# Reordering the state-space and the recurrent layer of a four-layer float32 program, and holding each layer's first weight splits behind the second token tile's copy

## The chip, the core and the metric

The program runs on one core of a Trainium2 chip. TensorE (PE) multiplies, with its weight loads on a row of their own (PEld); VectorE (DVE), ScalarE (ACT) and GpSimd (POOL) do the elementwise work, and SyncE (SP) issues the transfers from HBM. The metric is the device time of one execution, in microseconds.

## What is computed

256 tokens of width 1024 go through a first block (attention and a mixture of 16 experts) and a second block of four layers. Only the second block is touched: a state-space layer (SSD), a convolutional feed-forward layer (FFN 0), a gated linear recurrence (LRU) and FFN 1. All of it is float32. Cut to what matters:

```python
# SSD, 4 groups of 8 heads, 2 chunks of 128 tokens
cs = cumsum(dt * a); decay_in = exp(cs[l] - cs[s]) below the diagonal
y  = (C B^T * decay_in) @ (x*dt) + (C @ state) * exp(cs) + d_skip * x
g  = y * silu(z); g *= rsqrt(mean(g*g, over the 512 columns of a group)) * w
out = g @ w_out
# LRU, 10 blocks of 128 columns
x = dwconv(proj_x); gx, ga = sigmoid(blockwise x @ w_gx + b), sigmoid(x @ w_ga + b)
log_a = 8 * ga * log_sigmoid(lam); a = exp(log_a); m = sqrt(-expm1(2*log_a))
h_t = a_t * h_(t-1) + m_t * gx_t * x_t; out = (h * gelu(proj_y)) @ w_out + b_out
```

## The kernel before

Weights come in pages of 1 MB (128x2048 float32) into five slots, by SP, in the order in which the program asks for them. A matrix product takes both factors apart into two float32r tiles, a high and a low part, and adds three products (`three`, L234 to L236). `split` does this for a page: ACT copies the high part (`wh`, L222), DVE subtracts (`wl`, L223); three slots hold split pages. `c_proj` multiplies one page of 256 columns (48 PE products of 256 columns), `down` one page of an output projection (24 products of 512 columns into four accumulators `ca`). Two PSUM tags `cm` and `cs` with two buffers each take all else.

Between layers, `next_layer` (L1192) normalizes each of two token tiles of 128 tokens: sums of squares on ACT, scaling, and then `turned` (L1136): eight PE transposes, a copy of one half on ACT and of the other on DVE (`hf`, L1143), the products of the next layer's first two pages directly in float32 (`lead`, L1149), and the high parts on ACT (L1152) and low parts on POOL (L1153) of the activations.

In `ssd` (L1332) the step sizes go through `softplus` (L1272, a POOL chain of some 20 small instructions); four pages give B and C, two pages per group give x (`x_group`) and two z (`z_group`). `scan(g)` (L1416) builds decays for four heads at a time: `csb` (L1442) spreads a cumulative sum over partitions by float32 products with a triangle of ones, one for each head; DVE or ACT subtract, ACT takes the exponential, DVE multiplies, PE forms `y`. `scan_end(g)` multiplies by silu(z) on POOL (L1483), squares on ACT (L1484), sums by PE (`ssq`, L1488), takes the root in 13 small DVE steps, spreads it by PE (`rb`) and splits the result (`ys`), its low part on POOL. `out_group(g)` is the output projection. The order of the text is: for each g, scan(g), x_group(g+1), z_group(g), scan_end(g), out_group(g-1).

In `lru` (L1517) four small products put the output bias into the accumulators (L1531), `softplus` runs over `lambda`; five pages give x, each followed by its convolution and by `gates` of the page before (L1544: two PE products on each of two gates, tanh and sigmoid on ACT, DVE); five pages give y. Then, in five pieces, exp and tanh on ACT, a square on POOL (L1593), one root for all (L1595), and for each piece a product, two scans (L1600), gelu (L1601) and a product on DVE; the split has its low part on POOL. Five `down` pages follow, the last three in one call.

The queue of an engine is not the text's order: the framework plans, by its own estimates of durations, which instruction of an engine comes next, with earlier text first among those that it takes to be ready. Each engine then runs its queue strictly in order. `tc.issue_after(i)` makes the planner put an instruction behind `i` in the queue of the same engine. The weight pages of later text can so be split ahead.

Of the kernel before, what the change touches and what calls it, by code (L numbers as in the profile page):

```python
# [9 lines left out]
F32 = mybir.dt.float32  # L10
# [25 lines left out]
for _n, _k in COLS:  # L36
# [8 lines left out]
    ("ident", 128), ("one", 1), ("iota", 256), ("tok", 2), ("tri", 128), ("eye16", 16),  # L45
]
# [14 lines left out]
def constants():  # L61
# [24 lines left out]
    put("eye16", (p == np.arange(16)[None]).astype(np.float32))  # L86
    put("one", np.ones((128, 1), np.float32))
# [77 lines left out]
def tile_model(ctx, tc, A, out):  # L165
# [970 lines left out]
    def turned(t, xg, hf, hi, lo, lead):  # L1136

        os_ = [(slice(None), slice(4 * b, 4 * b + 4), nat(t)) for b in range(2)]
        for b in range(2):
# [3 lines left out]
            (act.copy, dve.tensor_copy)[b](hf[os_[b]], ps.rearrange("p (k n) -> p k n", k=4))  # L1143
# [150 lines left out]

    lru_lead = [lambda j=j: wpage(A["lru_w_in_2"][0], 1280 + 256 * j, 256) for j in range(2)]
# [36 lines left out]
    def ssd(hx, acc_, led):  # L1332
        with ExitStack() as es:
# [6 lines left out]
            da = sp2.tile([128, 2, 32], F32, name="da")  # L1340
# [13 lines left out]
            u = sp2.tile([128, 64], F32, name="dtu")  # L1354
            dve.tensor_copy(u, ps[:, :64])
            r = softplus(sp2, u, [128, 64], "sp")
            pool.tensor_copy(dt, r.rearrange("p (t h) -> p t h", t=2))
            pool.tensor_tensor(da, dt, na[:, None, :].to_broadcast([128, 2, 32]), ALU.mult)
# [35 lines left out]
            for t in range(2):  # L1394
                with tc.issue_after(last_mm[0].ins):
                    pe.matmul(ps[:, 32 * t:32 * t + 32], lhsT=K("tri"), rhs=da[:, t], start=True, stop=True)
            pe.matmul(ps[:, 64:96], lhsT=K("one").to_broadcast([128, 128]), rhs=da[:, 0], start=True, stop=True)
            dve.tensor_copy(csn, ps[:, :64].rearrange("p (t h) -> p t h", t=2))
            dec = sp2.tile([128, 32], F32, name="dec")
# [16 lines left out]
            def scan(g):  # L1416
# [18 lines left out]
                for q in range(2):  # L1435
# [43 lines left out]
            def scan_end(g):  # L1479
                sq = xs[g]  # L1480
                for q in range(2):
                    qs = slice(2 * q, 2 * q + 2)
                    pool.tensor_tensor(zs[g][:, qs], zs[g][:, qs], xs[g][:, qs], ALU.mult)  # L1483
# [11 lines left out]
                for c in range(4):  # L1495
                    dve.scalar_tensor_tensor(zs[g][:, c], zs[g][:, c], C("ssd_norm_2", 4 * g + c), rb[:, :256],
                                             ALU.mult, ALU.mult)
                ys[g] = split(zs[g], sp3, "ys", 2, pool)
# [5 lines left out]

            for g in range(4):
# [11 lines left out]
    def lru(hx, led):  # L1517
        with ExitStack() as es:
# [8 lines left out]
            for n in range(2):  # L1527
                b_out = lp.tile([128, 2 * S], F32, name="b_out", tag="raw", bufs=2)[:1]
                sync.dma_start(out=b_out, in_=A["lru_b_out_2"][:, 512 * n:512 * n + 512])
# [7 lines left out]
            hb = lp.tile([128, 20], F32, name="hb")  # L1537
            dve.tensor_scalar(hb[:, :10], C("lru_b_gx_2", 0, 10), 0.5, None, ALU.mult)
            xb = lp.tile([128, 10, S], F32, name="xb")
            yb = ly.tile([128, 10, S], F32, name="yb")  # L1540
            gx = lp.tile([128, 10, S], F32, name="gx")
            la = lp.tile([128, 10, S], F32, name="la")

            def gates(i):  # L1544
                for j, g in enumerate((gx, la)):
                    ps = cs("lgate")
                    for c in range(2):
                        ch = 2 * i + c
                        pe.matmul(ps[:, 256 * c:256 * c + 256], lhsT=wg[j][:, ch], rhs=xb[:, ch], start=True, stop=True)  # L1549
                    for c in range(2):  # L1550
                        ch = 2 * i + c
                        p_ = ps[:, 256 * c:256 * c + 256]
                        if j == 0:

                            act.activation(out=gx[:, ch], in_=p_, func=AF.Tanh, scale=0.5, bias=hb[:, ch:ch + 1])
                            dve.scalar_tensor_tensor(gx[:, ch], gx[:, ch], 1.0, xb[:, ch], ALU.add, ALU.mult)
                        else:
                            act.activation(out=la[:, ch], in_=p_, func=AF.Sigmoid, bias=C("lru_b_ga_2", ch))
                            dve.tensor_scalar(la[:, ch], la[:, ch], ls[:, ch:ch + 1], None, ALU.mult)

            for i in range(5):
# [9 lines left out]
                conv2(xb[:, 2 * i:2 * i + 2], raw, lambda c, a: C("lru_conv_w_2", 10 * a + 2 * i + c),  # L1571
                      lambda c: C("lru_conv_b_2", 2 * i + c), 4)
                if i:
                    gates(i - 1)

            def y_page(i):
                ps = cm("ly")
                c_proj(wpage(w, 256 * i, 256), ps, hx)
                for c in range(2):
                    ch = 2 * i + c  # L1580
                    dve.tensor_scalar(yb[:, ch], ps[:, 256 * c:256 * c + 256], C("lru_b_in_2", ch), None, ALU.add)

            y_page(0)
# [11 lines left out]
            act.activation(out=la, in_=la, func=AF.Sqrt)  # L1595
            for o in range(0, 10, 2):
                os_ = slice(o, o + 2)
                dve.scalar_tensor_tensor(gx[:, os_], gx[:, os_], 0.5, la[:, os_], ALU.mult, ALU.mult)
                for ch in (o, o + 1):
                    dve.tensor_tensor_scan(la[:, ch], xb[:, ch], gx[:, ch], 0.0, ALU.mult, ALU.add)  # L1600
                act.activation(out=yb[:, os_], in_=yb[:, os_], func=AF.Gelu_apprx_tanh)  # L1601
                dve.tensor_tensor(yb[:, os_], yb[:, os_], la[:, os_], ALU.mult)
            items = []
            for b in range(5):
                pr_ = split(yb[:, 2 * b:2 * b + 2], ly, "ls", 3, pool)
                items.append((rpage(A["lru_w_out_2"][0], 256 * b), [sl(pr_, lambda u: u[:, a]) for a in range(2)]))
                if b < 2:
                    down(acc_, [items.pop()], False, False)
            es2.close()
            lp = es.enter_context(tc.tile_pool(name="lru_out", bufs=1, reuse_waits="tile"))  # L1610
            root_table(lp, pr_[0].bitcast(F32)[:, 0, 0:1])
            down(acc_, items, False, True, lp)
# [29 lines left out]
```

## Time and profile before

| | us |
|---|---|
| median of 3 runs (2313.93 to 2317.94) | 2314.22 |
| the profiled execution, its own time | 2311.94 |
| its span, first to last instruction | 2310.1 |
| first block (to the end of the experts) | 0 to 1386 |
| SSD, with the passage into it | 1386 to 1634 |
| passage and FFN 0 | 1634 to 1910 |
| passage into LRU, LRU | 1910 to 2028 |
| passage and FFN 1 | 2028 to 2310 |

The span is 1.84 us shorter than the profiled execution's time, and that execution is 2.28 us below the median. A window view gives the busy time of each engine in a stretch and, under PEclk, TensorE's granted clock as a share of 2.4 GHz (0.50 is 1.2 GHz). Records of PE overlap, since matmuls are pipelined; the pace of a stream is read from the distance of starts.

### The profile page before, as it was taken

What the parts mean: (1) busy time and instruction counts of PE and PEld (TensorE: products, weight loads), DVE (VectorE), ACT (ScalarE), POOL (GpSimd) and SP (SyncE); (2) the same over time, 40 slices, a digit from 0 to 9 for tenths busy, and PEclk for the clock granted to TensorE, in tenths of its full rate; (3) what the DMA queues carried; (4) which work ended last, traced back from release to release, by engine and by line L of the source; (5) the groups of instructions that cost most, each with busy time, mean ns of one, the idle gap of its engine ahead of it and who ended that gap; (6) DMA issues with size and microseconds to landing.
All of it is one profiled execution on the core that took longest, in us unless ns stands there. A gap on an engine that the chain in (4) does not pass through costs nothing. (4 is left out here: it accounts for less than half of the span.)

```text
span 2310.1 us, 30319 instructions
## 1 busy us (share of the span) xinstructions
PE 1921.2 (83%) x12819; PEld 1341.3 (58%) x12819; DVE 996.5 (43%) x1473; ACT 806.4 (35%) x1190; POOL 268.8 (12%) x209
## 2 busy tenths in 40 slices
PE   7999999988665656656565669999999999899998
PEld 5989999933111111111111118887888888788887
DVE  8866664331000000000000007765677766777775
ACT  3445454311000000000000006664666667666664
POOL 0100032100000000000000003112322222222221
PEclk9999999999878787877888789999999999999999
DMA  9357666699999999999999997333466546456562
GB/s 321 109 188 262 227 219 203 238 372 427 426 427 426 425 428 426 427 426 427 425 428 426 427 414 250 103 111 127 148 199 192 188 149 206 146 175 190 184 199 82
DMA packets 211167, 645.22 MB, mean 279 GB/s; under 512 B 8148, under 2 KB 162132, under 8 KB 178390
## 3 DMA queue, kind: packets, MB, share of 16 engines
q1 hardware_dynamic: 211032, 643.28, 73.5%
q8 instruction: 101, 1.65, 0.3%
q14 instruction: 34, 0.28, 0.0%
HBM read 641.94 MB, written 1.05 MB: 278 GB/s over the span
## 5 line engine op out<-in xcount | busy, mean ns | idle before, releaser
L223 DVE TENSOR_TENSOR wl<-page,wh 128x2048 fp32r<-128x2048 f32 (+2 forms) x191 | 436.3, 2286 | 207.1 <-ACT wh L222 206.9
L1084 PE MATMUL gu<-epage,xeT 128*32 128x512 f32 x2048 | 318.4, 739 | 198.0 <-DMA epage<-in_w_gu 198.0
L222 ACT CAST wh<-page 128x2048 fp32r<-128x2048 f32 (+2 forms) x191 | 356.9, 1873 | 174.9 <-issue 46.2
L1236 PE MATMUL up<-hb,wh 128*128 128x512 f32 x960 | 331.6, 396 | 0.0
L1084 PEld LDWEIGHTS gu<-epage,xeT 128*32 128x32 f32 x2048 | 60.9, 123 | 435.2 <-DMA epage<-in_w_gu 326.0
L1087 ACT ACTIVATE hid<-gu 128x512 f32<-128x512 f32 x16 | 9.6, 597 | 786.6 <-PE gu L1084 786.6
L1105 PE MATMUL dn<-epage,hidT 128*32 128x512 f32 x1024 | 168.7, 788 | 104.4 <-DMA epage<-in_w_dn 95.5
L1239 PE MATMUL up<-hb,wl 128*128 128x256 f32 x960 | 248.0, 279 | 0.0
L1088 DVE TENSOR_TENSOR hid<-hid,gu 128x512 f32<-128x512 f32 x16 | 11.0, 688 | 490.6 <-PE gu L1084 490.6
L1236 PEld LDWEIGHTS up<-hb,wh 128*128 128x128 f32 x960 | 173.3, 188 | 33.4
L1239 PEld LDWEIGHTS up<-hb,wl 128*128 128x128 f32 x960 | 180.9, 188 | 10.4
L1105 PEld LDWEIGHTS dn<-epage,hidT 128*32 128x32 f32 x1024 | 31.5, 129 | 226.0 <-DMA epage<-in_w_dn 155.5
L1108 DVE TENSOR_TENSOR ye<-dn,gt 128x512 f32<-128x512 f32 x16 | 11.1, 692 | 286.9 <-PE dn L1105 286.9
L1269 DVE SCALAR_TENSOR_TENSOR cv<-ups,cols,cv 128x255 f32<-128x255 f32 x240 | 118.1, 502 | 28.8 <-ACT cv L1264 26.0
L278 POOL TENSOR_SCALAR iq<-ssq 128x1 f32<-128x1 f32 x16 | 8.0, 500 | 1002.0 <-ACT x L267 958.1
L234 PE MATMUL qk<-hh,wh 128*128 128x256 f32 x384 | 109.9, 286 | 0.0
L235 PE MATMUL qk<-hl,wh 128*128 128x256 f32 x384 | 109.0, 284 | 0.0
L236 PE MATMUL qk<-hh,wl 128*128 128x256 f32 x384 | 108.7, 283 | 0.0
L234 PE MATMUL ca<-wh,hdh 128*128 128x512 f32 x256 | 99.9, 390 | 0.0
L236 PE MATMUL ca<-wh,hdl 128*128 128x512 f32 x256 | 99.7, 390 | 0.0
L235 PE MATMUL ca<-wl,hdh 128*128 128x512 f32 x256 | 99.6, 389 | 0.0
L1264 ACT ACTIVATE cv<-ups,cols 128x256 f32<-128x256 f32 x120 | 71.1, 599 | 80.1 <-DVE ups L1244 79.9
(508 smaller groups left out, 3742.4 us busy)
## 6 DMA issues: line engine op xcount, KB each, us to landing
epage<-in_w_gu SPq DMA_DIRECT2D x102, 2048.0 KB, 29.5
epage<-in_w_dn SPq DMA_DIRECT2D x51, 2048.0 KB, 29.5
page<-in_ffn_w_up SPq DMA_DIRECT2D x64, 1024.0 KB, 5.6
epage<-in_w_gu SPq DMA_DIRECT2D x52, 1024.0 KB, 34.3
page<-in_w_in SPq DMA_DIRECT2D x46, 1024.0 KB, 5.7
page<-in_ffn_w_down SPq DMA_DIRECT2D x32, 1024.0 KB, 4.8
epage<-in_w_dn SPq DMA_DIRECT2D x26, 1024.0 KB, 34.3
page<-in_w_ada SPq DMA_DIRECT2D x24, 1024.0 KB, 8.9
```

The source lines that it names most:

```text
L222: act.copy(hi[p_], v[p_])
L223: (lo or dve).tensor_tensor(lw[p_], v[p_], hi[p_], ALU.subtract)
L234: pe.matmul(ps, lhsT=ah, rhs=bh, start=first and k == 0, stop=False)
L235: pe.matmul(ps, lhsT=ah, rhs=bl, start=False, stop=False)
L236: last_mm[0] = pe.matmul(ps, lhsT=al, rhs=bh, start=False, stop=last and k == n - 1)
L1084: pe.matmul(gu[i][32 * j:32 * j + 32, :], lhsT=xeT[:, k, 32 * e:32 * e + 32], rhs=pg[i][:, 512 * j:512 * j + 512], start=(k == 0), stop=(k ...
L1105: pe.matmul(pd[32 * q:32 * q + 32, :], lhsT=hT[:, 2 * c2 + cp, j, :], rhs=pg[c2][:, o:o + 512], start=(j == 0 and c2 == 0), stop=(j == 3 a ...
L1108: dve.tensor_tensor(ye, pd, gt2, ALU.mult)
L1236: wide = lambda: pe.matmul(ps, lhsT=wh[:, k, cc], rhs=hx[k][2], start=(k == 0), stop=(k == 7))
L1239: last_mm[0] = pe.matmul(ps[:, :256], lhsT=wl[:, k, cc], rhs=hx[k][0], start=False, stop=False)
L1264: act.activation(out=y[:, c], in_=ps[:, 256 * c:256 * c + 256], func=AF.Identity, scale=wcol(c, taps - 1), bias=bcol(c))
L1269: dve.scalar_tensor_tensor(y[:, c, o:], ps[:, 256 * c:256 * c + S - o], wcol(c, j), y[:, c, o:], ALU.mult, ALU.add)
```

## The change

- `split` issues the first three page splits after each passage behind ACT's `hf` copy of the second token tile.
- SSD: `z_group(0)` comes ahead of the first scan, and `z_group(g+1)` behind `scan_end(g)`; `out_group(0)` behind z_group(2), `out_group(1)` inside the last scan, `out_group(2)` behind the last scan_end. `csb` is one float32r product of 512 columns in place of four float32 ones; its right side is made once, ahead of the scans. The product with silu(z) goes from POOL to DVE, the normalized result has its own tile, and the last group's low part goes to DVE in two pieces.
- LRU: softplus of `lambda` is done in SSD's softplus, as ten more columns. The bias becomes four float32r products, behind the last gates. The gates come one projection later. The exponentials are queued behind the last sigmoid; the first three gelu pieces come at once behind the root, the last two y pages come behind it too, with gelu taken from PSUM. Square and low parts go from POOL to DVE.

```diff
+    behind_ = [None, 0]
     def split(v, pl=None, tag="w", bufs=None, lo=None, parts=1):
...
+        ahead = tag == "w" and behind_[1] > 0
+        behind_[1] -= ahead
         for i in range(parts):
-            act.copy(hi[p_], v[p_])
+            with tc.issue_after(behind_[0].ins) if ahead else ExitStack():
+                act.copy(hi[p_], v[p_])
             (lo or dve).tensor_tensor(lw[p_], v[p_], hi[p_], ALU.subtract)
@@ turned
-            (act.copy, dve.tensor_copy)[b](hf[os_[b]], ps.rearrange("p (k n) -> p k n", k=4))
+            c_ = (act.copy, dve.tensor_copy)[b](hf[os_[b]], ps.rearrange("p (k n) -> p k n", k=4))
+            if b == 0 and t == 1:
+                behind_[:] = [c_, 3]
@@ ssd
+            u = sp2.tile([128, 74], F32, name="dtu")
+            pool.tensor_scalar(u[:, 64:], C("lru_lambda_2", 0, 10), -1.0, None, ALU.mult)
...
+            r = softplus(sp2, u, [128, 74], "sp")
+            pool.tensor_scalar(lru_c[:, :10], r[:, 64:], -8.0, None, ALU.mult)
...
+            for t in range(2):
+                pr = cs("csr")[:, :128]
+                pe.matmul(pr, lhsT=da[:, t].rearrange("p a h -> p (a h)"), rhs=K("tri"), start=True, stop=True)
+                v_ = sp2.tile([128, 128], F32R, name="csv", tag="csv", bufs=2)
+                act.copy(v_, pr)
+                dve.tensor_tensor(v_[32:64], pr[32:64], v_[32:64], ALU.subtract)
+                bd = sp2.tile([128, 4, 128], F32R, name="csd", tag="csd", bufs=2)
+                dve.tensor_tensor(bd, v_[:, None, :].to_broadcast([128, 4, 128]),
+                                  K("mod4")[:, :, None].to_broadcast([128, 4, 128]), ALU.mult)
+                rows.append(bd.rearrange("p u l -> p (u l)"))
@@ scan
-                        for u_ in range(4):
-                            pe.matmul(ps[:, 128 * u_:128 * u_ + 128],
-                                      lhsT=da[:, t, hb + u_:hb + u_ + 1].to_broadcast([128, 128]), rhs=K("tri"),
-                                      start=True, stop=True)
+                        pe.matmul(ps, lhsT=of4[:, hb // 4:hb // 4 + 1].to_broadcast([128, 128]), rhs=rows[t],
+                                  start=True, stop=True)
@@ scan_end
-                    pool.tensor_tensor(zs[g][:, qs], zs[g][:, qs], xs[g][:, qs], ALU.mult)
+                    dve.tensor_tensor(zs[g][:, qs], zs[g][:, qs], xs[g][:, qs], ALU.mult)
...
-                ys[g] = split(zs[g], sp3, "ys", 2, pool)
+                ys[g] = split(sq, sp3, "ys", 2, dve if g == 3 else pool, parts=2 if g == 3 else 1)
@@ order of the groups
+            z_group(0)
             for g in range(4):
                 scan(g)
                 if g < 3:
                     x_group(g + 1)
-                z_group(g)
+                else:
+                    out_group(1)
                 scan_end(g)
-                if g:
-                    out_group(g - 1)
+                if g < 3:
+                    z_group(g + 1)
+                if g == 1:
+                    out_group(0)
+            out_group(2)
@@ lru
-                for t in range(2):
-                    pe.matmul(acc_[t][n], lhsT=K("one")[:1].to_broadcast([1, 128]), rhs=b_out, start=True, stop=False)
-            lam = lp.tile([128, 10], F32, name="lam")
-            dve.tensor_scalar(lam, C("lru_lambda_2", 0, 10), -1.0, None, ALU.mult)
-            ls = softplus(lp, lam, [128, 10], "lam")
-            dve.tensor_scalar(ls, ls, -8.0, None, ALU.mult)
+            def biases():
...
+                for n in range(2):
+                    for t in range(2):
+                        pe.matmul(acc_[t][n], lhsT=one_r, rhs=b_r[:, 512 * n:512 * n + 512], start=True, stop=False)
...
-                if i:
-                    gates(i - 1)
+                for j in {2: [0], 3: [1], 4: [2, 3]}.get(i, []):
+                    gates(j)
...
+            y_page(0, False)
             gates(4)
-            for i in range(1, 5):
-                y_page(i)
+            biases()
+            for i in range(1, 3):
+                y_page(i, False)
             for o in range(0, 10, 2):
                 os_ = slice(o, o + 2)
-                act.activation(out=xb[:, os_], in_=la[:, os_], func=AF.Exp)
+                with tc.issue_after(last_sig[0].ins):
+                    act.activation(out=xb[o // 2], in_=la[:, os_], func=AF.Exp)
...
-                pool.tensor_tensor(q, xb[:, os_], xb[:, os_], ALU.mult)
+                dve.tensor_tensor(q, xb[o // 2], xb[o // 2], ALU.mult)
...
+            root = act.activation(out=la, in_=la, func=AF.Sqrt)
+            with tc.issue_after(root.ins):
+                act.activation(out=yb[:, :6], in_=yb[:, :6], func=AF.Gelu_apprx_tanh)
...
+                if b > 2:
+                    y_page(b, True)
...
+                hi, lo = (lp.tile([128, 2, S], F32R, name="ls" + n, tag=n, bufs=5) for n in ("gx", "xb"))
+                act.copy(hi, yb[:, os_])
+                dve.tensor_tensor(lo, yb[:, os_], hi, ALU.subtract)
```

## Rows read from the trace of the kernel before

**Rows 1.** The page: each engine's busy time, share of the span, instructions

```profile
PE 1921.2 (83%) x12819; PEld 1341.3 (58%) x12819; DVE 996.5 (43%) x1473; ACT 806.4 (35%) x1190; POOL 268.8 (12%) x209
```

**Rows 2.** Windows by stage: stretch, its length, busy time by engine, PEclk, DMA share, GB/s

```profile
1386.00:1407.00 21.00, 17.23 (x120) 14.04 (x120) 15.35 (x19) 15.06 (x32) 9.37 (x12) 1.00 0.70 219
1442.00:1634.00 192.00, 181.03 (x1282) 159.19 (x1280) 118.62 (x218) 107.53 (x145) 31.49 (x14) 0.96 0.34 110
1910.00:1936.00 26.00, 22.55 (x156) 19.25 (x155) 13.84 (x19) 14.77 (x25) 10.78 (x24) 0.93 0.63 195
1936.00:1991.00 55.00, 54.90 (x425) 53.67 (x425) 47.34 (x77) 52.70 (x70) 8.17 (x6) 1.00 0.64 216
1991.00:2028.00 37.00, 30.07 (x120) 24.03 (x119) 25.76 (x28) 14.61 (x23) 7.36 (x8) 0.86 0.28 86
2028.00:2049.00 21.00, 18.45 (x147) 17.88 (x146) 13.80 (x13) 12.97 (x20) 7.28 (x5) 0.92 0.38 125
```

**Rows 3.** Waits of PE, 1442 to 1634: total us, times, longest

```profile
PE ssq L1488 <- ACT xs L1484: 6.9, 5, 2.0
```

**Rows 4.** Waits of PE, 1910 to 2049

```profile
PE ca L235 <- DVE wl L223: 6.9, 1, 6.9
PE lead L1149 <- DVE hf L1143: 3.1, 1, 3.1
PE lead L1149 <- ACT hf L1143: 2.9, 3, 2.2
```

**Rows 5.** Timeline of PE: start, us, instruction; the stream of csb, then one of 512 columns

```profile
1449.13 2.00 PE L1442 MATMUL csb<-kc,da 128*128 128x128 f32 x16
1450.89 0.36 PE L235 MATMUL xbc<-hb,wh 128*128 128x256 f32 x1
...
1888.47 0.39 PE L235 MATMUL ca<-wl,hdh 128*128 128x512 f32 x1
1888.70 0.39 PE L236 MATMUL ca<-wh,hdl 128*128 128x512 f32 x1
```

**Rows 6.** Groups by form, 1442 to 1634: busy us, mean ns, idle before, releasers

```profile
L223 DVE TENSOR_TENSOR wl<-page,wh 128x2048 fp32r<-128x2048 f32 x19 | 43.3, 2287 | 18.8 <-ACT wh L222 18.6
...
L1483 POOL TENSOR_TENSOR zs<-zs,xs 128x512 f32<-128x512 f32 x8 | 20.8, 2596 | 129.2 <-ACT zs L1384 106.6 <-ACT wh L222 13.1 <-DVE xs L1476 9.6
L1442 PE MATMUL csb<-kc,da 128*128 128x128 f32 x128 | 18.4, 282 | 0.0
...
L1454 DVE TENSOR_TENSOR scr<-scr,cb 128x512 f32<-128x512 f32 x16 | 11.0, 691 | 7.2 <-ACT scr L1453 7.0
L223 POOL TENSOR_TENSOR ysl<-zs,ysh 128x1024 fp32r<-128x1024 f32 x4 | 9.6, 2393 | 39.7 <-ACT ysh L222 20.0 <-issue 19.7
...
L1428 DVE TENSOR_TENSOR xd<-xdt,dec 128x512 f32<-128x512 f32 x4 | 4.7, 1169 | 0.0
```

**Rows 7.** Windows: the end of group 0, the clock in it, the scan of group 1

```profile
1467.00:1485.00 18.00, 16.04 (x121) 15.84 (x122) 7.72 (x17) 6.91 (x7) 4.16 (x2) 0.91 0.38 117
1481.00:1486.00 5.00, 5.00 (x32) 5.00 (x31) 2.57 (x13) 2.14 (x2) 0.00 (x0) 0.67 0.15 50
1485.00:1511.00 26.00, 24.39 (x208) 21.70 (x207) 21.57 (x38) 20.01 (x30) 3.65 (x2) 1.00 0.23 69
```

**Rows 8.** Timelines of ACT and DVE in three passages between layers

```profile
1400.83 0.58 ACT L1143 COPY hf<-tT 128x512 f32<-128x512 f32 x1 [2.56 <-PE tT L1142]
...
1923.26 1.21 DVE L1536 TENSOR_SCALAR r<-r 128x10 f32<-128x10 f32 x1 [5.04 <-POOL r L1289]
1924.39 0.68 DVE L1143 COPY hf<-tT 128x512 f32<-128x512 f32 x1
...
2035.80 3.68 ACT L222 CAST wh<-page 128x2048 fp32r<-128x2048 f32 x2
2039.39 0.57 ACT L1143 COPY hf<-tT 128x512 f32<-128x512 f32 x1
```

**Rows 9.** Group by form, 1910 to 2050: the bias products of LRU

```profile
L1531 PE MATMUL ca<-b_out,kc 1*128 1x512 f32 x8 | 4.0, 614 | 0.0
```

More of the change, by code (lines that the diff above doesn't have):

```diff
@@ L86, in constants @@
     put("eye16", (p == np.arange(16)[None]).astype(np.float32))
+    put("mod4", (p % 4 == np.arange(4)[None]).astype(np.float32))
+    put("of4", ((p < 64) & (p % 32 // 4 == np.arange(8)[None])).astype(np.float32))
     put("one", np.ones((128, 1), np.float32))
@@ L1293, in up_lead @@
         return [lambda j=j: wpage(A["ffn_w_up_2"][i], 4096 * j, 256) for j in range(2)]
+    lru_c = cp.tile([128, 20], F32, name="lru_c")
+    pool.tensor_scalar(lru_c[:, 10:], C("lru_b_gx_2", 0, 10), 0.5, None, ALU.mult)
     lru_lead = [lambda j=j: wpage(A["lru_w_in_2"][0], 1280 + 256 * j, 256) for j in range(2)]
@@ L1339, in ssd @@
             dt = sp2.tile([128, 2, 32], F32, name="dt")
-            da = sp2.tile([128, 2, 32], F32, name="da")
+            da = sp2.tile([128, 2, 4, 32], F32, name="da")
             ps = led[0]
@@ L1395, in ssd @@
                 with tc.issue_after(last_mm[0].ins):
-                    pe.matmul(ps[:, 32 * t:32 * t + 32], lhsT=K("tri"), rhs=da[:, t], start=True, stop=True)
-            pe.matmul(ps[:, 64:96], lhsT=K("one").to_broadcast([128, 128]), rhs=da[:, 0], start=True, stop=True)
+                    pe.matmul(ps[:, 32 * t:32 * t + 32], lhsT=K("tri"), rhs=da[:, t, 0], start=True, stop=True)
+            pe.matmul(ps[:, 64:96], lhsT=K("one").to_broadcast([128, 128]), rhs=da[:, 0, 0], start=True, stop=True)
             dve.tensor_copy(csn, ps[:, :64].rearrange("p (t h) -> p t h", t=2))
+            of4 = sp2.tile([128, 8], F32R, name="of4")
+            act.copy(of4, K("of4"))
+            rows = []
+            for t in range(2):
[8 more added lines that the diff above has]
+                rows.append(bd.rearrange("p u l -> p (u l)"))
             dec = sp2.tile([128, 32], F32, name="dec")
@@ L1526, in lru @@
             acc_ = accs()
[L1527 to L1539 removed]
+            ls, hb = lru_c[:, :10], lru_c[:, 10:]
+            def biases():
+                one_r = lp.tile([64, 128], F32R, name="one_r")
+                act.copy(one_r, K("one")[:64].to_broadcast([64, 128]))
+                b_out = lp.tile([64, D], F32, name="b_out")
+                pool.memset(b_out, 0.0)
+                for i in range(2):
+                    sync.dma_start(out=b_out[32 * i:32 * i + 1], in_=A["lru_b_out_2"])
+                b_r = lp.tile([64, D], F32R, name="b_r")
+                act.copy(b_r, b_out)
+                pool.tensor_tensor(b_r[32:64], b_out[32:64], b_r[32:64], ALU.subtract)
+                for n in range(2):
+                    for t in range(2):
+                        pe.matmul(acc_[t][n], lhsT=one_r, rhs=b_r[:, 512 * n:512 * n + 512], start=True, stop=False)
+            xb, gx = ([lp.tile([128, 2, S], F32, name=n, tag=n, bufs=5) for _ in range(5)] for n in ("xb", "gx"))
             yb = ly.tile([128, 10, S], F32, name="yb")
[L1541 removed]
             la = lp.tile([128, 10, S], F32, name="la")
+            last_sig = [None]
             def gates(i):
[L1545 removed]
+                for j in range(2):
                     ps = cs("lgate")
@@ L1548, in gates @@
                         ch = 2 * i + c
-                        pe.matmul(ps[:, 256 * c:256 * c + 256], lhsT=wg[j][:, ch], rhs=xb[:, ch], start=True, stop=True)
+                        with tc.issue_after(last_mm[0].ins):
+                            pe.matmul(ps[:, 256 * c:256 * c + 256], lhsT=wg[j][:, ch], rhs=xb[i][:, c], start=True, stop=True)
                     for c in range(2):
@@ L1580, in y_page @@
                     ch = 2 * i + c
-                    dve.tensor_scalar(yb[:, ch], ps[:, 256 * c:256 * c + 256], C("lru_b_in_2", ch), None, ALU.add)
-            y_page(0)
+                    p_, b_ = ps[:, 256 * c:256 * c + 256], C("lru_b_in_2", ch)
+                    if gelu:
+                        act.activation(out=yb[:, ch], in_=p_, func=AF.Gelu_apprx_tanh, bias=b_)
+                    else:
+                        dve.tensor_scalar(yb[:, ch], p_, b_, None, ALU.add)
+            y_page(0, False)
@@ L1609, in lru @@
+            item = lambda b: (rpage(A["lru_w_out_2"][0], 256 * b), [sl(pr_[b], lambda u: u[:, a]) for a in range(2)])
+            for b in range(2):
+                down(acc_, [item(b)], False, False)
+            root_table(cp, pr_[4][0].bitcast(F32)[:, 0, 0:1])
+            down(acc_, [item(b) for b in range(2, 5)], False, True)
             es2.close()
-            lp = es.enter_context(tc.tile_pool(name="lru_out", bufs=1, reuse_waits="tile"))
-            root_table(lp, pr_[0].bitcast(F32)[:, 0, 0:1])
```

42 lines of the change are left out of this document (18 added, 24 removed).

## The prediction

> **What bounds the kernel now.** The page comes first [rows 1]: PE is busy for 83% of the span, DVE 43%, ACT 35%, so it is PE's idle time and its slow stretches that can be won, and PE's own work. The windows by stage say where they lie [rows 2]. From 1936 to 1991, in the middle of LRU, PE is busy 54.90 of 55 us at full clock: nothing is to be had there but fewer products. SSD (192 us) has 11.0 us without PE, and a granted clock of 0.96. The end of LRU (37 us) has 6.9 us without PE at 0.86. The two passages around LRU have 3.5 and 2.6 us without PE at 0.93 and 0.92. The waits of PE name the causes: in SSD the squares of a group's end come late (6.9 us in five waits) [rows 3]; in LRU one wait of 6.9 us for the low part of a page, 3.1 us for DVE's copy in the passage into it, and 2.9 us for ACT's copies, of which 2.2 us at one go [rows 4]. A wait costs more than itself: after the idle time in group 0's end the clock falls to 0.67 for five microseconds [rows 7], which is 5 x 0.33 = 1.7 us more.
>
> A change of under 0.2% (4.6 us) can't be told from none here.
>
> **Part by part.**
>
> **csb.** Sixteen records start between 1449.13 and 1450.89, one each 0.11 us [rows 5]; 128 of them [rows 6] take 14.1 us of PE. Sixteen products of 512 columns, at 0.23 us between starts [rows 5], take 3.7. Making the right side adds four records of 128 columns: 0.4. Net 10.0. PE is busy 181 of 192 us there [rows 2], so I take 94% of it: **-9.4** (ends -5 and -10). The other new steps are three ACT copies and four DVE instructions, each bounded by 0.69 us, the DVE product of 512 elements [rows 6], 4.8 us in all. They lie between the last B/C page and the first csb, beside the products of z's first two pages (96 x 0.12 = 11.5 us, at half of the 0.23); without that cover they would cost their 4.8.
>
> **The end of a group.** POOL takes 2.60 us for half of the product with silu(z), DVE 0.69 for that shape [rows 6]. The last half is on the way to the squares, so 1.9 us go at each of four ends, about what each wait is long (2.0 at most) [rows 3]. With the wait goes the slow stretch: 6.9 us and four times 1.7 make 13.5. SSD's idle time and lost clock together are 11.0 + 192 x 0.04 = 18.7 [rows 2], so there is room for that. The next that can be late is the chain of roots behind the squares; it then has z_group(g+1) beside it (11.5 us of PE), and in the last group out_group(2) (48 x 0.23 = 11). I take **-12** (ends -4, where the next link waits, and -16).
>
> First the row: DVE's `xd`, a product of the 0.69 us kind, takes 1.17 us in the mean of four [rows 6], which are 1.9 us too many in all. The Trainium skill, in "SBUF — State Buffer", section "Who interferes with whom", says that a DVE instruction with two SBUF inputs waits for a whole GpSimd instruction that reads SBUF. By that rule a moved product that met one of the three low parts left on POOL (2.39 us each) would wait for it, at most 7.2 us together, and the sum below would be 24.7 in place of 31.9.
>
> **DVE's new load, and the scans' lost cover.** DVE gets eight products (5.5 us), the last group's low part (two of 0.69) and the 2.8 us of above: 9.7 us on top of 118.6 in 192. That is hidden on the whole, but not evenly. The scan of group 1 now takes 26 us, DVE 21.6 of them [rows 7], and PE had two x and two z pages beside it. After the change z stands behind scan_end: the scan has some 6 us of PE of its own (an estimate: the stretch's 24.4 less 0.9 a csb stream saved and four pages' products as far as they lie in it) and two x pages, 11.5, so 17.5 us against about 22 of DVE. Four scans lose 0 us if the planner pulls z's products ahead (two `cm` buffers and three split slots allow one group) and 4.5 each, 18, if it doesn't. In the trace a later page's product stands right behind the csb stream [rows 5], so I take a value nearer to nothing: **+5**.
>
> **Holding the splits.** Three ACT copies a passage are queued behind `hf`; behind them stand the tile's two casts, then the first product of the layer. In the passage into SSD: hf from 1400.83 for 0.58 [rows 8], two casts of as much, 1.84 for the copy (two in 3.68) [rows 8], 2.29 for the low part [rows 6]: 1406.7. PE is meanwhile on 48 float32 products of the lead pages ((120 - 8 - 16)/2 records [rows 2], 5.3 us at 0.11) until about 1407; in the other passages on 64, 7 us. So the hold costs 0 (end: 2 us each, where DVE or the `softplus` feed comes between). A page slot comes free up to 5 us later, so its transfer does too, but PE needs 5.8 us (48 x 0.12) for each held page, and the DMA share is 0.28 to 0.70 in these stretches [rows 2]: nothing.
>
> **Passage into LRU.** DVE's `hf` copy stands behind the last step of softplus, which waits 5.0 us for POOL's chain [rows 8]; softplus now runs in SSD, where its POOL chain only gets ten columns more and two small instructions. The 3.1 us wait goes, and with it the lost clock (26 x 0.07 = 1.8). Eight records of the bias take 4.0 us [rows 9]; four products of 512 columns take 0.9, later: 3.1. Together 8.0, I take **-7** (ends -5 and -8). Its transfers move behind y's first page on SP, two short rows; POOL clears and subtracts beside 24 us of PE.
>
> **LRU's middle.** Gates one projection later and fewer table loads on ACT (52.7 of 55 busy) win nothing while PE is full [rows 2]: **0**.
>
> **LRU's end.** 120 products at 0.23 are 27.6 of the 37 us: 9.4 us lost to the late page split and the half clock behind it. DVE was the one that came late. It loses the stretched products beside POOL and four of ten bias additions, and gets five squares and five low parts (10 x 0.69). ACT loads the gelu table once. But y's fourth and fifth page now stand behind the root. I take about half: **-5** (ends 0 and -9).
>
> **Passage into FFN 1.** Two page copies (3.68 us) stand ahead of `hf` [rows 8] and PE waits 2.2 us [rows 4]; with the clock (21 x 0.08 = 1.7) that is 3.9. Held, they are gone from there: **-3.5** (ends -2 and -4). Into FFN 0 ACT had idle time for them; 0.
>
> **Sum.** -9.4 - 12 + 5 + 0 - 7 + 0 - 5 - 3.5 = -31.9 us against the profiled execution, 2311.94: 2280.0. That execution lies 2.28 below the median, so 2282.
>
> **The rivals.**
>
> **The scans become DVE's.** The +5 is +18, and SSD wins 3.4 instead of 16.4: 2295. For it: DVE at 21.6 of 26 us with the same x pages [rows 7]. Against it: csb comes 0.6 us sooner four times a scan, and DVE is busy just 7.7 of 18 us in a group's end, so there is room to shift its work. The Trainium skill, in "Perfetto Trace Analysis", section "Optimizing Scalar/DVE Operations", speaks against the move too: where DVE is saturated, work should rather go to ScalarE or GpSimd, and between DVE and GpSimd moving may not help. The trace agrees for the scans and not for the ends. Chance 0.20.
>
> **The new order isn't what is queued.** The planner orders by its own estimates, so the moved groups may stand where they stood; only replaced instructions count: csb 9.4, the passage into LRU 7. 2298. Chance 0.08.
>
> **Slower: PE stands still in every scan.** If each scan, with x alone beside it, is stretched to the sum of its DVE work and ACT's links, some 30 us (22 + 8), SSD from 1442 to 1634 becomes: z 11.5, four scans 120, four ends 18 - 3.8 = 14.2 each, two output groups outside 22, eight slow restarts of 1.7: 224 against 192 plus the 6 ahead of it. That is +26, less 15.5 of LRU: +10.5, 2325 at the median. It decides from 27 us a scan on (with LRU's gain used up). For it: the queues are in order, so one late DVE result stops PE with pages ready behind it. Against it: 26 us now, with more DVE work inside [rows 7]. Chance 0.08.
>
> **How the numbers follow.** The forecast has 0.64: 2282, its own range 2267 (all good ends: 10 + 16 + 8 + 9 + 4 = 47) to 2292. To leave out no more than 2 in 10, the range goes up to the two rivals at 2295 and 2298 with a little of their bad ends: 2267 to 2301. Faster by over 0.2%: 0.64, 0.16 of the DVE rival and 0.07 of the order rival, 0.87. Within 0.2%: the bad ends of these two, 0.05. Slower: 0.08.
>
> **What would show it.** In the profile after: 16 csb records of 512 columns 0.23 apart; no wait of `ssq` for ACT, and SSD's clock at 0.98 or more; SSD's stretch shorter by 16 us; the passage into LRU near 18 us without the wait for `hf`; LRU's end at 32; no page copy ahead of `hf` in any passage. Wrong would be: waits of PE for `scr` or `xd` in the scans with DVE full (the first rival); first products of a layer waiting for `wl` (the hold costs); a new wait in LRU for the low part of y's fourth page.

## The result, and the profile after the change

The changed kernel takes 2276.41 us (median of four runs, 2275.1 to 2277.32) against 2315.3 for the kernel before beside it: a ratio of 0.9831, 95% interval 0.9819 to 0.9842, so it is faster by 38.9 us. The profiled executions, on which the sum was made, are 2311.94 and 2275.1: 36.8 us, where 31.9 were forecast.

The first 1393 us are the same code but for one POOL instruction of 0.3 us, so I cut the rest at PE's records, from the first record of one tile to the first of the next. Profiles of code that is alike in a stage agree on most middle and late stages within 0.2 us: FFN 0 takes 257.29 to 257.33 in ten of them, SSD's body 176.6 in the five that leave it alone and keep its clock. LRU's middle is looser (56.1 to 56.5, and 57.4 in run 3, which does not touch it), the start of the transposes into SSD lies anywhere from 1393.2 to 1398.6, and the passage into SSD takes 13.8 to 15.2. So the stages, not the totals, carry the readings below.

| stage (us) | before | after | difference | forecast |
|---|---|---|---|---|
| up to the transposes into SSD | 1393.2 | 1393.7 | +0.5 | 0 |
| passage into SSD | 13.8 | 13.8 | 0 | 0 |
| to the running sums (`csn`) | 29.1 | 29.5 | +0.4 | 0 |
| SSD's body, to the transposes into FFN 0 | 200.0 | 176.6 | -23.3 | -16.4 |
| passage into FFN 0, to `up` | 19.0 | 17.0 | -2.0 | 0 |
| FFN 0 | 255.1 | 257.3 | +2.2 | 0 |
| passage into LRU, to `lx` | 25.5 | 17.1 | -8.4 | -7 |
| LRU's middle, to the last product of y | 55.0 | 56.2 | +1.2 | 0 |
| LRU's end | 37.5 | 31.3 | -6.2 | -5 |
| passage into FFN 1 | 20.7 | 17.1 | -3.6 | -3.5 |
| FFN 1, to its last product | 254.9 | 257.1 | +2.2 | 0 |
| the rest | 6.4 | 6.5 | +0.2 | 0 |

The windows by stage of the changed kernel, as in [rows 2] (stretch, length, busy time of PE, PEld, DVE, ACT, POOL, PEclk, DMA share, GB/s):

```profile
1437.00:1613.00 176.00, 168.96 (x1222) 146.89 (x1222) 130.09 (x243) 103.69 (x150) 12.09 (x6) 1.00 0.39 126
1888.00:1905.00 17.00, 16.38 (x144) 15.87 (x142) 11.82 (x11) 12.80 (x23) 9.09 (x6) 1.00 0.77 236
1961.00:1992.00 31.00, 28.52 (x123) 22.45 (x123) 23.77 (x30) 15.27 (x25) 1.52 (x3) 1.00 0.33 102
1992.00:2009.00 17.00, 16.38 (x142) 15.73 (x141) 11.36 (x11) 11.10 (x19) 7.63 (x5) 1.00 0.10 23
```

The granted clock is 1.00 in all four; it was 0.96, 0.93, 0.86 and 0.92. Of the waits named in [rows 3, 4], the one for `ssq` is gone, the one for `wl` is 1.1 us and none for `hf` is over 0.4; the longest wait of any kind from SSD's body to FFN 1 is 1.7. The waits of PE in the changed kernel, first SSD's body, then LRU's end (total, times, longest):

```profile
PE ca L243 <- ACT wh L231: 3.2, 2, 1.7
PE st L1466 <- DVE xd L1462: 1.5, 1, 1.5
PE z L243 <- DVE cvs L1280: 1.5, 1, 1.5
```

```profile
PE ca L245 <- DVE lsxb L1661: 1.4, 1, 1.4
PE ca L244 <- DVE wl L232: 1.1, 1, 1.1
```

DVE is busy for 130 of SSD's 176 us, and PE waits for it there twice for 1.5 us and once for 0.2.

### The profile page after: what moved, and what is told of

Read it like the earlier page. It is cut to its first block, busy times and chain, and to the rows that moved or that the text cites. A ratio compares the mean times of both kernels' runs of the same rounds, so it can differ in the third digit from the quotient of the medians.

```text
span 2273.3 us, 30086 instructions
## 1 busy us (share of the span) xinstructions
PE 1903.4 (84%) x12707; PEld 1317.6 (58%) x12707; DVE 1001.5 (44%) x1486; ACT 790.4 (35%) x1181; POOL 247.4 (11%) x176
## 4 chain that ended last, share of the span: by engine, by line
PE 56%; DMA 38%; DVE 3%; ACT 2%; issue 1%; SPq 0%; DVEq 0%; ACTq 0%
DMA epage<-in_w_gu 25%; DMA epage<-in_w_dn 13%; PE up L1247 10%; PE up L1250 5%; PE ca L245 4%; PE ca L244 3%; PE ca L243 3%; PE lead L1160 2%; PE qk L243 2%; PE qk L245 2%; PE qk L244 2%; PE gu L1093 1%; PE v L245 1%; PE v L244 1%; PE v L243 1%; PE xbc L243 1%
```

## The experiments

Times are given as the ratio to the kernel before, with its 95% interval, and as the stage that the edit touches. All change the changed kernel but one: the second of experiment 1 puts the same unused columns into the kernel before. "Run 3" and the like are the experiments by their numbers here.

**1. Why did the FFNs become slower?** Neither has a wait of PE, and the products are the same. The timeline of PE in FFN 0 (start, us), before and after:

```profile
1666.35 0.39 PE L234 MATMUL ca<-wh,hdh 128*128 128x512 f32 x1
1666.58 0.39 PE L235 MATMUL ca<-wl,hdh 128*128 128x512 f32 x1
1666.81 0.39 PE L236 MATMUL ca<-wh,hdl 128*128 128x512 f32 x1
1667.03 0.39 PE L234 MATMUL ca<-wh,hdh 128*128 128x512 f32 x1
```

```profile
1641.98 0.40 PE L243 MATMUL ca<-wh,hdh 128*128 128x512 f32 x1
1642.22 0.39 PE L244 MATMUL ca<-wl,hdh 128*128 128x512 f32 x1
1642.45 0.39 PE L245 MATMUL ca<-wh,hdl 128*128 128x512 f32 x1
1642.68 0.40 PE L243 MATMUL ca<-wh,hdh 128*128 128x512 f32 x1
```

The triple of a down projection goes from 0.68 to 0.70 us. An FFN has 128 of them, of which the last 16 take 0.69 to 0.71 in both kernels; the other 112 make 2.2 us. The `up` products keep their pace. Twelve more columns of constants and LRU's small tile moved every tile behind them, so the first guess was the place.

```diff
-    ("mod4", 4), ("of4", 8),
+    ("mod4", 4), ("of4", 8), ("pad", 8),
```

> The changed kernel with eight unused columns (32 bytes a partition) more at the end of its table of constants: all tiles allocated behind it lie 32 bytes later, and the split parts of the pages start at multiples of 64 bytes again, as before the change (in the changed kernel at 32 past one). Theory, place: three products of a down projection (512 columns) take 680 ns again and not 700; each FFN stage is 2.2 us shorter, SSD and LRU together 1 to 2 us, so 2270 to 2272 us. Rival, order: the FFNs became slower because the held splits move their ACT queue or because other code lies ahead; then nothing changes, 2276, and the triple stays at 700 ns.

> The kernel before with the same eight unused columns, which put its split parts at 32 past a multiple of 64 bytes. Theory, place: the triple of a down projection goes from 680 to 700 ns, each FFN stage gets 2.2 us longer, the whole 5 to 7 us: 2320 to 2322. Rival, order: no change, 2315.

Both fell. Ratios 0.9833 (0.9819 to 0.9846) and 0.9999 (0.999 to 1.0009): the triple stays at 0.70 in the one and 0.68 in the other. But this pad moves both operands together. By the tile addresses of the two programs, the weights' and the activations' parts lie at the same remainder of 512 bytes in the kernel before and in its shifted form; in the changed kernel and its padded form the weights' lie 352 bytes on from the activations', counted in that remainder. Moving one alone tells:

```diff
-    lru_c = cp.tile([128, 20], F32, name="lru_c")
+    lru_c = cp.tile([128, 108], F32, name="lru_c")
...
```

> The changed kernel with the small tile of LRU constants 88 columns (352 bytes a partition) longer, not used: the activations' split parts (hd, ys, ls) lie at the same remainder of 512 bytes as the weights' split parts again, as before the change; in the changed kernel, and in the first run with eight more columns of constants, 352 bytes apart, in the kernel before and its shifted run 0. Theory, relative place: the triple of a down projection takes 680 ns and not 700, each FFN stage 255.1 and not 257.3 us, and with SSD and LRU 6 us in all: 2270 to 2272. Rival: the place plays no part, and something else in the changed program slows these products: triple 700, 2276.

Ratio 0.981 (0.9796 to 0.9823), where the change alone has 0.9831 (0.9819 to 0.9842). The timeline of PE in FFN 0 of this run:

```profile
1647.58 0.39 PE L243 MATMUL ca<-wh,hdh 128*128 128x512 f32 x1
1647.81 0.39 PE L244 MATMUL ca<-wl,hdh 128*128 128x512 f32 x1
1648.04 0.39 PE L245 MATMUL ca<-wh,hdl 128*128 128x512 f32 x1
1648.26 0.39 PE L243 MATMUL ca<-wh,hdh 128*128 128x512 f32 x1
```

The FFNs take 255.1 and 254.9 us again. The theory holds for them, and the rival is out. LRU's end won 0.6. SSD's body did not win its share: it takes 177.6 us in this profile, in which the granted clock falls behind one of its waits (0.89 over 15 us there, 1.00 in the changed kernel; see experiment 2). The total fell 4.1 us and not 6.

**2. The hold.**

```diff
-                behind_[:] = [c_, 3]
+                behind_[:] = [c_, 0]
```

> The changed kernel without the hold: no split waits for the second token tile's copy. Theory: the passage into FFN 1 gets its 3.6 us back (17.1 to 20.7), the passage into FFN 0 the 2.0 us that the prediction had put at nothing (17.0 to 19), the passage into LRU under 2: 2282 to 2284 in all. Rival: the passages got shorter because the work ahead of them ends in another order, and the hold does nothing: 2276 to 2278.

Ratio 0.9855 (0.984 to 0.987). The passages grow by 1.9 (FFN 0), 1.7 (LRU) and 1.9 us (FFN 1), and SSD's body by 1.5: the sum expected, split otherwise. The 1.5 is not shown to be the hold's. PE's waits in SSD's body are the same with and without it, and behind the same wait of 1.5 us for a page's high part the granted clock fell in this profile and stayed full in the changed kernel's; in the last profile of experiment 1 it fell too, with the hold in place. The window of 15 us about that wait, without the hold and in the changed kernel:

```profile
1505.00:1520.00 15.00, 13.47 (x107) 12.68 (x106) 12.06 (x30) 6.73 (x9) 0.00 (x0) 0.89 0.45 141
1503.00:1518.00 15.00, 13.47 (x118) 12.73 (x118) 12.70 (x32) 7.72 (x10) 0.00 (x0) 1.00 0.46 141
```

So the hold is worth 5.6 us in the three passages. ACT in the passage into FFN 0 (start, us, what ended the idle time), in the kernel before, without the hold, and with it:

```profile
1641.25 3.68 ACT L222 CAST wh<-page 128x2048 fp32r<-128x2048 f32 x2
1647.30 0.58 ACT L1143 COPY hf<-tT 128x512 f32<-128x512 f32 x1 [2.37 <-PE tT L1142]
```

```profile
1624.64 3.69 ACT L231 CAST wh<-page 128x2048 fp32r<-128x2048 f32 x2
1628.23 0.58 ACT L1152 COPY hf<-tT 128x512 f32<-128x512 f32 x1
```

```profile
1622.94 0.59 ACT L1152 COPY hf<-tT 128x512 f32<-128x512 f32 x1 [1.54 <-PE tT L1151]
1623.42 1.90 ACT L231 CAST wh<-page 128x2048 fp32r<-128x2048 f32 x1
```

Before, ACT was idle for 2.4 us ahead of `hf`, as the prediction said: PE's first 64 lead products took 8.9 us, at a granted clock of 0.92 over the passage, behind a wait of 1.9 us ahead of the transposes. In the changed kernel that wait is gone, the clock is 1.00 and the products take 7.25 us; without the hold the two page copies are then late, and PE waits 2.2 us for `hf`. The hold pays there because another edit took away the idle time that covered the copies.

**3. csb alone undone.**

```diff
-                        pe.matmul(ps, lhsT=of4[:, hb // 4:hb // 4 + 1].to_broadcast([128, 128]), rhs=rows[t],
-                                  start=True, stop=True)
+                        for u_ in range(4):
+                            pe.matmul(ps[:, 128 * u_:128 * u_ + 128],
+                                      lhsT=da[:, t, 0, hb + u_:hb + u_ + 1].to_broadcast([128, 128]), rhs=K("tri"),
+                                      start=True, stop=True)
```

> The changed kernel with each head's row of running sums made by four float32 products of 128 columns again, in place of one of 512; the right sides of the new form are still made, so only the products differ. Theory: 10 us of PE come back, nearly all on the path since PE is busy 171 of 178 us there: plus 9.4, 2286. Rival: with z's products elsewhere the scans are paced by DVE and ACT, and the four products fit in their gaps: plus 0 to 4, 2276 to 2280.

Ratio 0.9882 (0.9866 to 0.9897). SSD's body is 188.0 and not 176.6: 11.3 us, all of the products' difference and a little more (two of the four `xd` take 2.28 us here and 0.68 in the changed kernel; experiment 4 says why). The rival is out.

**4. The product and the order of the groups, each alone and both.**

```diff
-                    dve.tensor_tensor(zs[g][:, qs], zs[g][:, qs], xs[g][:, qs], ALU.mult)
+                    pool.tensor_tensor(zs[g][:, qs], zs[g][:, qs], xs[g][:, qs], ALU.mult)
```

> The changed kernel with the product with silu(z) back on POOL (two halves of 2.60 us in each group's end). Theory, the engine pays: each of the four ends comes 1.9 us later and loses the clock behind it, plus 8 to 13 us, SSD's body 185 to 190, 2284 to 2289. Rival, the order pays: z's pages of the next group stand beside the end now and hide 1.9 us more, plus 0 to 3, 2276 to 2279.

```diff
-            z_group(0)
             for g in range(4):
                 scan(g)
                 if g < 3:
                     x_group(g + 1)
-                else:
-                    out_group(1)
+                z_group(g)
                 scan_end(g)
-                if g < 3:
-                    z_group(g + 1)
-                if g == 1:
-                    out_group(0)
-            out_group(2)
+                if g:
+                    out_group(g - 1)
```

> The changed kernel with the groups queued as before the change (z of a group behind its own scan, the output products of a group behind the next one's end). Theory, the order pays: the roots and the low part of an end have little of PE beside them again, plus 6 to 12 us, SSD's body 183 to 189, 2282 to 2288. Rival, the prediction's own step, in which the new order costs the scans 5 us of cover: minus 5 to 0, 2271 to 2276.

> The changed kernel with both the old order of SSD's groups and the product with silu(z) on POOL. In the new order the product on POOL made SSD's body 2.0 us shorter (176.6 to 174.7), in the old order on DVE it took 182.6. Theory, the two are one step: in the old order the product is on the way and POOL's 1.9 us a half cost 4 to 8 us, SSD's body 185 to 189, 2285 to 2289; then csb, order and engine together explain the 23.3 us. Rival, they add: 180.6, 2280, and some 6 us of SSD's gain come from elsewhere.

SSD's body in us (ratios 0.982, 0.9855 and 0.9906 for the three; intervals 0.9807 to 0.9834, 0.984 to 0.987, 0.9891 to 0.9921):

| | product on POOL | product on DVE |
|---|---|---|
| old order | 193.8 | 182.6 |
| new order | 174.7 | 176.6 |

In the old order the move to DVE is worth 11.3 us; in the new one it costs 2.0. The new order is worth 5.9 us on top of the move and 19.2 without it. The first expectation fell on both sides (POOL is better, not equal). The order's theory held at the edge of its range (5.9 us for 6 to 12), and with both undone the body costs 17.2 us, more than its theory's 8 to 12; the passage into FFN 0 behind it then takes 20.2 us instead of 17.0, at a clock of 0.83.

One path leads from the kernel before to the changed one: 200.0 us, then 193.8 with the new csb and the small edits beside it, 182.6 with the move, 176.6 with the order. These steps, 6.1, 11.3 and 5.9 us, make the 23.3 that the body won. From another starting point they differ: csb is worth 11.3 in the new order (experiment 3), so the third text's sum of csb, order and engine comes to 28.5 us by the prices in these runs and does not explain the 23.3. The windows of the body with both undone, then with the order alone undone, show what goes with it, the granted clock at 0.94 and 0.98; it was 0.96 in the kernel before [rows 2]:

```profile
1437.00:1631.00 194.00, 182.05 (x1232) 157.82 (x1230) 128.08 (x238) 108.15 (x156) 28.59 (x14) 0.94 0.35 114
1441.00:1624.00 183.00, 172.65 (x1231) 150.30 (x1230) 136.73 (x246) 114.48 (x159) 9.45 (x6) 0.98 0.38 121
```

The waits of PE in SSD's body, old order with POOL, then old order with DVE:

```profile
PE ssq L1520 <- ACT xs L1516: 7.4, 5, 2.0
```

```profile
PE st L1466 <- DVE xd L1462: 6.2, 3, 2.9
PE ca L243 <- ACT ysh L231: 3.1, 1, 3.1
```

The first is [rows 3] again. The second has grown (1.5 us, once, in the changed kernel), and POOL's and DVE's timelines of that run say why:

```profile
1491.20 2.35 POOL L232 TENSOR_TENSOR ysl<-xs,ysh 128x1024 fp32r<-128x1024 f32 x1 [58.31 <-ACT ysh L231]
```

```profile
1453.67 0.68 DVE L1462 TENSOR_TENSOR xd<-xdt,dec 128x512 f32<-128x512 f32 x1
1491.66 2.44 DVE L1462 TENSOR_TENSOR xd<-xdt,dec 128x512 f32<-128x512 f32 x1
```

Three of the four `xd` fall on POOL's low part of the group before and take 2.28 to 2.72 us, 0.68 without it: 5.4 us in all. In the new order all four take 0.68. That is not shown to be the whole of the order's 5.9: the old order also has the wait of 3.1 us in the last group's end and the clock of 0.98, and the new one has waits for page copies (3.2) and for a convolution (1.5) that the old one does not have. No run takes these apart. The Trainium skill, "SBUF — State Buffer", section "Who interferes with whom", says that a DVE instruction with two SBUF inputs contends with a GpSimd instruction that reads SBUF; this run agrees.

The same meeting had made POOL's product late in the first place. POOL's first two halves in the kernel before, and DVE beside the second; then the second half in run 4 (new order, POOL):

```profile
1466.98 1.30 POOL L1483 TENSOR_TENSOR zs<-zs,xs 128x512 f32<-128x512 f32 x1 [42.81 <-ACT zs L1384]
1475.37 2.88 POOL L1483 TENSOR_TENSOR zs<-zs,xs 128x512 f32<-128x512 f32 x1 [7.08 <-ACT zs L1384]
```

```profile
1474.84 2.29 DVE L223 TENSOR_TENSOR wl<-page,wh 128x2048 fp32r<-128x2048 f32 x1 [3.82 <-ACT wh L222]
```

```profile
1475.16 1.28 POOL L1515 TENSOR_TENSOR zs<-zs,xs 128x512 f32<-128x512 f32 x1 [5.05 <-DVE xs L1508]
```

Alone the product takes 1.3 us; beside a page's low part on DVE it takes 2.9. In the new order it meets convolution steps instead, all eight halves take 1.28 to 1.61, and there is nothing left for a move to win. What the move loses there goes with the wait of 1.5 us for `xd`, which this run does not have.

**5. LRU's softplus back in LRU.**

```diff
-            ls, hb = lru_c[:, :10], lru_c[:, 10:]
+            lam = lp.tile([128, 10], F32, name="lam")
+            dve.tensor_scalar(lam, C("lru_lambda_2", 0, 10), -1.0, None, ALU.mult)
+            ls = softplus(lp, lam, [128, 10], "lam")
+            dve.tensor_scalar(ls, ls, -8.0, None, ALU.mult)
+            hb = lru_c[:, 10:]
```

> The changed kernel with LRU's softplus computed at LRU's start again, the bias products left in their new form and place. Theory: DVE's copy into hf waits for POOL's chain of the softplus again, and the passage into LRU (17.1 us) gets 3.1 to 4.9 us longer: 2279 to 2281. Rival: with the first splits held behind the copy the engines have room there, and the passage stays within 1 us of 17.1: 2276 to 2277.

Ratio 0.9868 (0.9853 to 0.9883); the passage takes 24.8 us, 7.6 more. DVE's timeline, and the wait of PE that follows:

```profile
1905.72 0.17 DVE L1568 TENSOR_SCALAR r<-r 128x10 f32<-128x10 f32 x1 [5.50 <-POOL r L1300]
1905.81 0.48 DVE L1200 TENSOR_SCALAR xg<-xg,iq 128x512 f32<-128x512 f32 x1
```

```profile
PE tT L1151 <- DVE xg L1200: 4.9, 1, 4.9
```

The chain stands one step earlier in DVE's queue than in [rows 8], ahead of the scaling that the transposes need. PE waits 4.9 us for it, 3.1 in the kernel before, and the granted clock of the passage is 0.86, 0.93 in the kernel before. The theory had the mechanism and too small a price; 7.6 us is the price in this queue, not what the chain cost in the kernel before.

**6. LRU's end, its two halves.**

```diff
-            for i in range(1, 3):
+            for i in range(1, 5):
                 y_page(i, False)
...
                 if b > 2:
-                    y_page(b, True)
+                    act.activation(out=yb[:, os_], in_=yb[:, os_], func=AF.Gelu_apprx_tanh)
```

> The changed kernel with y's fourth and fifth page projected ahead of the root again (bias by DVE, gelu by ACT behind the root), all else as changed. Theory, the pages are the cover of LRU's end: from the first product of x's third page to the transposes into FFN 1 it takes 87.4 us now and 92.4 before, and 3 to 5 us come back: 2279 to 2281. Rival, the products taken from POOL pay: 0 to 1 us, 2276 to 2277.

```diff
-                dve.tensor_tensor(q, xb[o // 2], xb[o // 2], ALU.mult)
+                pool.tensor_tensor(q, xb[o // 2], xb[o // 2], ALU.mult)
...
-                dve.tensor_tensor(lo, yb[:, os_], hi, ALU.subtract)
+                pool.tensor_tensor(lo, yb[:, os_], hi, ALU.subtract)
```

> The changed kernel with LRU's five squares and five low parts back on POOL, y's pages where the change put them. Theory, the pages are the cover: two pages (11.5 us of PE) hide what POOL takes longer, 0 to 2 us, 2276 to 2278. Rival, the engine pays: POOL's five low parts come one behind the other and PE waits for the first and the last, plus 3 to 6 us, 2279 to 2282.

Ratios 0.9834 (0.9821 to 0.9848) and 0.9846 (0.9832 to 0.9859); LRU's end takes 34.4 and 35.6 us, 3.1 and 4.4 more. The first number is what its theory said, yet not by its mechanism: on PE the last y page ends behind the root, next to the output products, in the kernel before as in all the others, so the pages are no new cover. What comes back is four bias additions on DVE (1.7 us), which now stand between the scans. In the second the theory fell and the rival's number held. The wait for the page's low part, 6.9 us in [rows 4] and 1.1 after, in these two:

```profile
PE ca L244 <- DVE wl L232: 2.8, 1, 2.8
```

```profile
PE ca L244 <- DVE wl L232: 4.4, 1, 4.4
```

Behind either wait the clock is 0.95 over the stage, 1.00 in the changed kernel, which makes 1.7 us of each. Why POOL's low parts cost DVE time is in POOL's and DVE's timelines of the second:

```profile
1966.71 3.49 POOL L1661 TENSOR_TENSOR lsxb<-yb,lsgx 128x512 fp32r<-128x512 f32 x2 [13.75 <-ACT lsgx L1660]
1974.96 1.46 POOL L1661 TENSOR_TENSOR lsxb<-yb,lsgx 128x512 fp32r<-128x512 f32 x1 [1.94 <-ACT lsgx L1660]
```

```profile
1964.39 0.67 DVE L1654 SCALAR_TENSOR_TENSOR gx<-gx,la 128x512 f32<-128x512 f32 x1
...
1967.36 1.69 DVE L1654 SCALAR_TENSOR_TENSOR gx<-gx,la 128x512 f32<-128x512 f32 x1
1968.97 1.78 DVE L1657 TENSOR_TENSOR yb<-yb,la 128x512 f32<-128x512 f32 x1
...
1975.28 3.29 DVE L232 TENSOR_TENSOR wl<-page,wh 128x2048 fp32r<-128x2048 f32 x1
```

Instructions of 0.67 and 2.29 us take a microsecond more beside POOL. The two halves sum to 7.5 where the stage won 6.2, so they do not simply add.

**7. What the runs point to: the place and the product on POOL together.**

The edits are the longer tile of experiment 1 and the product on POOL of experiment 4.

> The changed kernel with the longer tile of LRU constants (the split parts at the same remainder of 512 bytes) and the product with silu(z) on POOL. Theory: both gains stand beside each other, FFN stages at 255.1 and SSD's body near 174: 2269 to 2271. Rival: the faster down products leave POOL's product uncovered, and SSD's body stays at 176 to 178: 2272 to 2273.

2270.02 us, ratio 0.9801 (0.9788 to 0.9815), faster than the change alone (0.9819 to 0.9842). SSD's body takes 174.2 us, the FFNs 255.1 and 254.9. The theory held.

## Why the prediction was right

- **csb: right in kind, less in size.** -9.4 forecast, 6.1 measured on the path from the kernel before (experiment 4, with the small edits beside it), 11.3 in the new order (experiment 3), beyond the good end of -10. Sixteen products at 0.23 us were to take 3.7 us. In the changed kernel each stands alone between other products and not in a stream, as "what would show it" had it; the next start lies 0.23 to 0.63 us behind, 6.3 us for the sixteen.
- **The end of a group: right, in the old order.** -12 forecast, 11.3 measured there: the waits for the squares, 7.4 us, go, and the clock of the body rises from 0.94 to 0.98. (The two parts named for it, 6.9 and four times 1.7, make 13.7 and not 13.5.) In the new order POOL's products are no longer stretched, and the move costs DVE time instead (+2.0). The rule that the prediction named against the move, the Trainium skill's "Perfetto Trace Analysis", "Optimizing Scalar/DVE Operations" (between DVE and GpSimd it may not help), agrees with this 2.0, not with the 11.3.
- **"DVE's new load, and the scans' lost cover": +5 forecast, and this is the step that failed.** The new order, beside the moved product, is worth 5.9 us. I costed what z takes from the scans, and not which instructions of DVE and POOL would cease to meet, nor the wait of PE for the last group's split (3.1 us in the old order, 0.5 in the new). The meeting was in the prediction (1.9 us too many in [rows 6], up to 7.2 by the rule), as a risk of the moved product; in the old order it came true (5.4 us in three `xd`), and the new order removes it. From first `xT` to last `y`, scans take 18.8 to 22.4 us after, 22.7 to 25.9 before, so neither the DVE rival nor the slower one came.
- **The hold, "into FFN 0 ACT had idle time: 0": failed by 2.0 us.** The idle time was read in a trace where PE ran slow ahead of it. In the passage into LRU, where no gain of the hold was counted either, it is 1.7.
- **Passage into LRU: right (-7; measured -8.4).** In the kernel before, PE waits 3.1 us for `hf` [rows 4], the clock of 0.93 over 26 us is 1.8 more, and the eight bias products, here in PE's timeline, take 3.8 us to the next starts (1920.90 and 1935.72):

```profile
1919.85 1.12 PE L1531 MATMUL ca<-b_out,kc 1*128 1x512 f32 x2
1932.95 2.84 PE L1531 MATMUL ca<-b_out,kc 1*128 1x512 f32 x6
```

  That makes 8.7 for the 8.4; the new bias products cost 1.1 in LRU's middle, of its +1.2. The two parts can be added only together: with the chain back (experiment 5) the passage takes 24.8 us, 0.8 less than before, though the bias products stay away.
- **LRU's end: -5 forecast, -6.2 measured.** "About half" was a choice. That DVE came late, and that it loses additions and products stretched beside POOL, is what experiment 6 shows; that the pages stand behind the root adds nothing, since on PE they did before.
- **Passage into FFN 1: right (-3.5; -3.6), but only 1.9 of it is the hold's.** Without the hold PE waits the same 2.2 us; the clock's share of 1.6 stays won. That it does so because LRU no longer ends in a long wait is argued, not shown.
- **FFN: not in the prediction.** Two times +2.2 us from where tiles lie.

That the sum came within 5 us is partly luck. The order was off by 10.9 us, to the good; csb's 3.3 less than forecast and the FFNs' 4.4 gave most of that back. The rival by which the new order isn't what is queued is excluded by experiment 4: undoing the order changes the stage.

## What to carry to other kernels

Where an instruction's time varies between its instances, as POOL's product (1.3 or 2.9 us) and `xd` do, find what it meets first: the new order, which keeps the two apart among other things, was worth 19.2 us by itself where the move was worth 11.3, and after it the move was a loss. Give a price of one edit together with the state of the others, since csb was worth 6.1 or 11.3 us by the order around it. An idle time that hides something holds only at the pace of the trace it was read in; when an edit speeds up what comes before, look at each cover again. After any edit of tile sizes compare the pace of products that the edit doesn't touch.

## What was not expected of the hardware

**Products of 512 columns depend on where their two operands lie to each other.** With the weights' and activations' parts at the same remainder of 512 bytes, it is 227 ns between starts; 352 apart, 231 to 238. Moving both by 32 bytes changes nothing. Even the kernel before shows it: the last 16 triples of an FFN have their parts 64 bytes apart and take 0.69 to 0.71 us, in all three kernels. The `up` products stay at 233 ns in all. Only the distances 0, 64 and 352 were seen, so which modulus counts stays open.

**The same wait can lower the clock or not.** In the passage into FFN 1 PE stands still for 2.2 us in the kernel before and in the run without the hold. Windows over what follows, before and without the hold:

```profile
2037.00:2049.00 12.00, 9.83 (x73) 9.59 (x72) 7.31 (x5) 6.92 (x8) 3.81 (x2) 0.86 0.65 216
```

```profile
2008.00:2018.00 10.00, 7.83 (x70) 7.59 (x69) 5.09 (x3) 6.32 (x6) 3.81 (x2) 1.00 0.51 170
```

Before, LRU's end had its wait of 6.9 us ahead of that; without the hold it has none over 1.4. That this earlier wait decides is argued, not shown. The two windows of SSD in experiment 2 are closer still: the same wait of 1.5 us, with the same instructions of PE ahead of it, and then 0.89 or 1.00.

**DVE and POOL slow each other by the instruction.** One shape takes 1.28 to 3.45 us on POOL in the kernel before, and `xd` 0.68 to 2.72 on DVE in the old order with the product on DVE, by what lies beside it.
